# First load, zero products, evictions and normalisation times of a one-layer hybrid trunk

## The chip, the core and the metric

The kernel runs on one core of a Trainium2 chip. The time is the device time of one execution in microseconds (us); it was taken three times, and the median is the figure that counts. TensorE (PE) multiplies matrices, ScalarE (ACT) and VectorE (DVE) do elementwise work, GpSimd (POOL) adds a few tiles and issues some transfers, SyncE (SP) issues most of the transfers. Each engine executes its own list in order.

## The reference

One layer on x of 512 tokens by 2048 features, all in float32:

```
h  = rms_norm(x, g0)
P  = h @ w_in                    # 2048 x 5632, eleven blocks of 512 columns
y  = concat[A(P), B(P), C(P), D(P)]   # two attentions, a linear recurrence, a gated convolution
x  = x + rms_norm(y @ w_out, g1)      # w_out 2048 x 2048
h  = rms_norm(x, g2)
u  = causal_conv3(h @ w_up)           # w_up 2048 x 8192
x  = x + rms_norm((gelu(u1) * u2) @ w_down, g3)
```

rms_norm divides each token by the root of its mean square over the 2048 features and multiplies by a gain per feature.

## The kernel before

Activations stand features on partitions, tokens along the free axis, in 16 tiles of 128x512. So that float32 accuracy is kept, each operand is split into a rounded part hi and a remainder lo, and a product is made of three matmuls (hi·hi, hi·lo, lo·hi); in the half groups of w_out one matmul takes hi and lo of the activation together, 512 wide, and a second, 256 wide, takes lo of the weight.

Weights stream through `chunk` (line 95). A chunk is 128x1024 of a weight: SyncE loads w_raw (L105), ScalarE rounds it to w_hi (the cast, L106), VectorE subtracts to w_lo (L107). Each of the three has three buffers, so the load of chunk i waits for L107 of chunk i-3, and cast and subtraction of chunk i for the matmuls of chunk i-3. The first chunk is loaded and split in two pieces.

`group` (L132) makes 512 output columns: eight chunks into four PSUM banks, one u for each 128 columns. The last chunk goes bank by bank, and when a bank is complete its eviction `evac` is called with high priority; what `evac` returns is called afterwards in ordinary order. There are two pools of four banks, mm and pa. `tick` counts a quarter of a chunk, and `at(t, f)` puts work f beside tick t. TensorE's order is that of the program; the lists of the other engines are made by a scheduler, which takes high-priority work (loads, casts, subtractions) as early as it can.

Before the first product, TensorE multiplies a tile of zeros twenty times (L70 to L72; a float32 product is two passes, so 40 instructions). `load_x` (L266) loads x on SyncE, two feature tiles at a time after the first two, and splits them (L199 on ScalarE, L200 on VectorE). The squares of x go beside it: ScalarE squares (L282), VectorE sums them into vd (L284, L286). At tick 28, between chunk 6 and chunk 7 of the first group, `norm0` multiplies that sum with ones (L308) and makes the reciprocal root. The parameters (L298) are loaded late, and VectorE's small steps L375 to L392 (negb, la_s, la_q, la_m, lam, sp) need them.

w_out is four groups of columns. Groups 0 and 1 take all 512 tokens at once (PSUM tile of 128x512, both on mm); groups 2 and 3 take one half of the tokens, hf 0 then hf 1, group 2 on mm and group 3 on pa. Evictions of groups 0 and 1 are a scaled copy (L968) and squares (L838). Those of the halves add the two PSUM halves (ScalarE L978, VectorE L979), square (L838; GpSimd sums, L842) and scale by the gain (L964). When the sixteenth square of a half is out, `residual` is put six ticks later: ones times the sums (L852, two terms for hf 0, five for hf 1), a reciprocal root (L207, L210), multiplications (L876), for half of the tiles a transfer that adds onto xs (`accum_op`, L878, GpSimd's queue), for the others an add (L882). `residual` puts squares (L894, L896), `scaled` (L902, and a store of xs to x_d on SyncE, L904) and, 43 ticks on, `norm2` (L911 on TensorE, then L917 and the split L196, L197), which makes the operands of w_up.

Of the kernel before, what the change touches and what calls it, by code (L numbers as in the profile page):

```python
# [23 lines left out]
ALL = slice(0, S)  # L24
# [24 lines left out]
def trunk(ctx: ExitStack, tc: tile.TileContext, xT, params, consts, wgate, w_in, w_out, w_up0, w_up, w_dn, w_dns, out):  # L49
# [18 lines left out]
    idle = const.tile([P, P], F32, name="idle")  # L68
    V.memset(idle, 0.0)
    ps = pa_tile()[:, 0:P]  # L70
    for _ in range(20):
        T.matmul(ps, lhsT=idle, rhs=idle, start=True, stop=True)  # L72


# [20 lines left out]
    def chunk(src, pieces=1, place=None):  # L95
        with tc.high_priority(offset=AHEAD):
            raw = wp.tile([P, 2, S], F32, name="w_raw")
            if place is None:
                hi = wp.tile([P, 2, S], F32R, name="w_hi")
                lo = wp.tile([P, 2, S], F32R, name="w_lo")  # L100
            else:
                hi, lo = place[:, 0:2], place[:, 2:4]
            for i in range(pieces):
                sl = slice(2 * i // pieces, 2 * (i + 1) // pieces)
                w_load.append(nc.sync.dma_start(out=raw[:, sl], in_=src[:, sl]))  # L105
                w_split.append(A.copy(out=hi[:, sl], in_=raw[:, sl]))  # L106
                V.tensor_tensor(out=lo[:, sl], in0=raw[:, sl], in1=hi[:, sl].bitcast(F32), op=ALU.subtract)  # L107
        return hi, lo
# [701 lines left out]
    with ExitStack() as ph:  # L810
# [57 lines left out]
        def residual(hf):  # L868
# [14 lines left out]
            for n, q in enumerate((0, 2, 1, 3)):  # L883
                at(clock[0] + 19 + 5 * hf + 4 * n // 3, lambda n=n, q=q: squares(hf, q, acc, n == 0))
                at(clock[0] + 25 + 5 * hf + 2 * n, lambda q=q: scaled(hf, q))
            at(clock[0] + 43, lambda: norm2(hf, acc))

        def squares(hf, q, acc, first):

# [67 lines left out]
        def out_group(g, hfs, ts, pool_tile):  # L957
            def evac(u, ps):
                k = 4 * g + u
                if len(hfs) == 1:  # L960
                    m = mg[g][hfs[0]][:, u]
                    sum_of(m, ps)
                    last = ss1[hfs[0]].add(m)
                    A.activation(out=m, in_=m, func=AF.Copy, scale=gain(1, k))  # L964
                    if last:
                        at(clock[0] + 6, lambda: residual(hfs[0]))
                else:
                    A.activation(out=mg_t[g // 2][:, g % 2, :, u], in_=ps.rearrange("p (h t) -> p h t", h=2),  # L968
                                 func=AF.Copy, scale=gain(1, k))
                    for hf in hfs:  # L970
                        ss1[hf].add(ps[:, HALVES[hf]])
# [8 lines left out]


        for g in range(2):
            out_group(g, (0, 1), ALL, mm_tile)
        for hf in range(2):
            for g in range(2, 4):
                out_group(g, (hf,), HALVES[hf], mm_tile if g == 2 else pa_tile)
# [525 lines left out]
```

## Time and profile before

| what | value |
|---|---|
| three runs | 1744.21, 1743.61, 1743.55 us; median 1743.61 us |
| the profiled execution | 1741.86 us, of which the span in the profile is 1740.1 us |
| TensorE busy | 1730.1 us of the span, 9168 matmuls |
| VectorE, ScalarE, GpSimd busy | 1253.8, 905.8, 157.8 us |
| granted TensorE clock | full speed over the span |

The profile's engine times overlap. A wait in it is the idle time of an engine just before an instruction, put down to what ended it. On a busy engine each instruction's duration is longer than its step, since one starts before the last is out; what a row of equal instructions takes is read from start to start.

### The profile page before, as it was taken

To read this page: it belongs to the slowest core of one execution; us is meant where nothing else is said; L and a number is where in the kernel's file an instruction comes from. 1 tells how busy PE (TensorE), PEld (TensorE's weight loads), DVE (VectorE), ACT (ScalarE), POOL (GpSimd) and SP (SyncE) were. 2 spreads that over 40 slices of the span, in tenths; PEclk is the share of its full clock that TensorE was granted. 3 is DMA by queue.
4 is the path that set the end of the run, shared out by engine and by line. 5 is a ranking of instruction groups with operands and counts; after the bars stand their busy time and mean duration, and the time that the engine had idled before them with its cause. 6 is when DMAs were issued, how large, how long until landed. Compare 5 with 4: busy or idle time off the path is not lost.

```text
span 1740.1 us, 24385 instructions
## 1 busy us (share of the span) xinstructions
PE 1730.1 (99%) x9168; PEld 1482.5 (85%) x9168; DVE 1253.8 (72%) x1949; ACT 905.8 (52%) x1367; POOL 157.8 (9%) x227
## 2 busy tenths in 40 slices
PE   9999999999999999999999999999999999999998
PEld 8778888888888888899988888888888888888886
DVE  7885587666556425799898988888878887776335
ACT  6443577665334334776655555555555573334342
POOL 0000011100000011100011111111111001110120
PEclk9999999999999999999999999999999999999999
DMA  7224222242223625775789888888888768888322
GB/s 258 84 99 147 92 79 79 79 158 97 85 86 97 230 97 181 233 234 180 208 230 243 236 224 247 225 230 223 228 239 226 210 198 232 217 201 296 102 91 97
DMA packets 96014, 304.43 MB, mean 175 GB/s; under 512 B 10356, under 2 KB 14708, under 8 KB 95896
## 3 DMA queue, kind: packets, MB, share of 16 engines
q1 hardware_dynamic: 79768, 245.19, 42.1%
q0 software_dynamic: 15552, 56.63, 17.4%
q8 instruction: 72, 1.18, 0.3%
q10 hardware_dynamic: 576, 1.05, 0.2%
q14 instruction: 46, 0.38, 0.1%
HBM read 262.45 MB, written 21.24 MB: 163 GB/s over the span
## 4 chain that ended last, share of the span: by engine, by line
PE 92%; DVE 3%; DMA 2%; ACT 2%; issue 1%; SPq 0%; POOL 0%; ACTq 0%; DVEq 0%; POOLq 0%
PE mm L164 32%; PE mm L1113 27%; PE mm L1118 14%; PE pa L164 5%; PE pa L156 2%; PE mm L128 2%; PE mm L130 2%; PE mm L129 2%; PE mm L156 1%; PE pa L611 1%; DMA w_raw<-in_w_out_dram 1%; DVE w_lo L107 1%; DVE vd L286 1%; PE pa L718 1%; ACT w_hi L106 0%
## 5 line engine op out<-in xcount | busy, mean ns | idle before, releaser
L107 DVE TENSOR_TENSOR w_lo<-w_raw,w_hi 128x1024 fp32r<-128x1024 f32 (+1 forms) x195 | 238.5, 1224 | 234.6 <-PE mm L164 117.3
L106 ACT CAST w_hi<-w_raw 128x1024 fp32r<-128x1024 f32 (+1 forms) x195 | 203.5, 1044 | 264.0 <-PE mm L164 174.1
L164 PE MATMUL mm<-a,w_hi 128*128 128x512 f32 (+1 forms) x1504 | 338.2, 375 | 0.0
L164 PEld LDWEIGHTS mm<-a,w_hi 128*128 128x128 f32 x1504 | 266.7, 188 | 50.9 <-issue 1.8
L1113 PE MATMUL mm<-a,w_hi 128*128 128x512 f32 x1088 | 272.6, 392 | 0.0
L1081 ACT CAST w_hi<-w_raw 128x1024 fp32r<-128x1024 f32 x145 | 152.3, 1050 | 196.0 <-PE mm L1113 154.9
L1113 PEld LDWEIGHTS mm<-a,w_hi 128*128 128x128 f32 x1088 | 195.6, 189 | 35.3 <-issue 0.2
L1082 DVE TENSOR_TENSOR w_lo<-w_raw,w_hi 128x1024 fp32r<-128x1024 f32 x145 | 177.0, 1221 | 29.9 <-ACT w_hi L1081 29.3
L164 PE MATMUL mm<-a,w_lo 128*128 128x512 f32 (+1 forms) x752 | 180.4, 377 | 0.0
L1118 PEld LDWEIGHTS mm<-a,w_lo 128*128 128x128 f32 x1088 | 148.4, 190 | 10.6
L1118 PE MATMUL mm<-a,w_lo 128*128 128x256 f32 x1088 | 151.7, 282 | 0.0
L164 PEld LDWEIGHTS mm<-a,w_lo 128*128 128x128 f32 x752 | 131.8, 189 | 22.3
L1113 PE MATMUL mm<-xs,w_hi 128*128 128x512 f32 x576 | 144.3, 392 | 0.2 <-DVE ub L1179 0.2
L1081 ACT CAST w_hi<-mg 128x1024 fp32r<-128x1024 f32 x82 | 85.6, 1044 | 85.0 <-PE mm L1113 82.5
L1113 PEld LDWEIGHTS mm<-xs,w_hi 128*128 128x128 f32 x576 | 103.6, 189 | 19.0 <-DVE ub L1179 0.4
L1082 DVE TENSOR_TENSOR w_lo<-mg,w_hi 128x1024 fp32r<-128x1024 f32 x82 | 100.1, 1220 | 21.4 <-ACT w_hi L1081 21.4
L1113 PE MATMUL mm<-mg,w_hi 128*128 128x512 f32 x352 | 88.1, 392 | 0.0
L1118 PEld LDWEIGHTS mm<-xs,w_lo 128*128 128x128 f32 x576 | 78.6, 190 | 5.6
L1179 DVE TENSOR_TENSOR ub<-ub,mm 128x256 f32<-128x256 f32 x196 | 81.2, 414 | 0.0
L1118 PE MATMUL mm<-xs,w_lo 128*128 128x256 f32 x576 | 80.3, 282 | 0.0
L1281 DVE TENSOR_TENSOR m<-m,mm 128x256 f32<-128x256 f32 x112 | 46.5, 416 | 37.0 <-PE mm L1118 37.0
L1113 PEld LDWEIGHTS mm<-mg,w_hi 128*128 128x128 f32 x352 | 63.3, 189 | 11.3
(332 smaller groups left out, 2709.1 us busy)
## 6 DMA issues: line engine op xcount, KB each, us to landing
w_raw<-in_w_up_dram SPq DMA_DIRECT2D x115, 512.0 KB, 5.3
w_raw<-in_w_in_dram SPq DMA_DIRECT2D x87, 512.0 KB, 3.4
mg<-in_w_up_dram SPq DMA_DIRECT2D x54, 512.0 KB, 4.4
w_raw<-in_w_out_dram SPq DMA_DIRECT2D x48, 512.0 KB, 3.6
w_raw<-in_w_dn_dram SPq DMA_DIRECT2D x32, 512.0 KB, 4.2
mg<-in_w_up_dram POOLq DMA_DIRECT2D x27, 512.0 KB, 7.8
w_raw<-in_w_up_dram POOLq DMA_DIRECT2D x27, 512.0 KB, 8.9
w_raw<-mg POOLq DMA_DIRECT2D x27, 512.0 KB, 6.0
```

Of the source, the lines that this page charges most:

```text
L106: w_split.append(A.copy(out=hi[:, sl], in_=raw[:, sl]))
L107: V.tensor_tensor(out=lo[:, sl], in0=raw[:, sl], in1=hi[:, sl].bitcast(F32), op=ALU.subtract)
L128: T.matmul(ps, lhsT=sh, rhs=mh, start=first, stop=False)
L129: T.matmul(ps, lhsT=sh, rhs=ml, start=False, stop=False)
L156: T.matmul(pss[u][:, 0:256] if low else pss[u].rearrange("p (a t) -> p a t", a=2), lhsT=(wh, wl)[low][:, kk, us], rhs=both[k][:, 0, ts] if ...
L164: T.matmul(pss[u], lhsT=a, rhs=b, start=c == 0 and kk == 0 and not low and i == 0, stop=False)
L1081: w_split.append(A.copy(out=by4(hi), in_=v))
L1082: V.tensor_tensor(out=by4(lo), in0=v, in1=by4(hi).bitcast(F32), op=ALU.subtract)
L1113: T.matmul(ps.rearrange("p (a t) -> p a t", a=2), lhsT=hi[:, k * P:(k + 1) * P], rhs=tops[name][k], start=first and k == 0, stop=False, **kw)
L1118: T.matmul(ps[:, 0:256], lhsT=lo[:, k * P:(k + 1) * P], rhs=tops[name][k][:, 0], start=False, stop=k == 7, **kw)
L1179: taken.append(V.tensor_tensor(out=t, in0=t, in1=ps[:, 256:512], op=ALU.add))
L1281: V.tensor_tensor(out=t, in0=t, in1=part, op=ALU.subtract if i else ALU.add)
```

## The change

Five edits. (1) The very first weight piece is loaded by ScalarE's queue, all others by SyncE's as before. (2) Ten zero products in place of twenty. (3) In the half groups the squares and the scaled copy are returned by `evac` and so are issued in ordinary order; only the sum of the two PSUM halves stays at high priority. (4) The group with g = 1 of w_out takes its four banks from pa. (5) `residual` stands eight ticks after the last square and `norm2` 44 ticks after `residual`, in place of 6 and 43.

```
@@ -68,7 +68,7 @@
-    for _ in range(20):
+    for _ in range(10):
         T.matmul(ps, lhsT=idle, rhs=idle, start=True, stop=True)
@@ -102,7 +102,9 @@
-                w_load.append(nc.sync.dma_start(out=raw[:, sl], in_=src[:, sl]))
+                queue = nc.sync if w_load else nc.scalar
+                w_load.append(queue.dma_start(out=raw[:, sl], in_=src[:, sl]))
@@ -883,7 +885,7 @@
-            at(clock[0] + 43, lambda: norm2(hf, acc))
+            at(clock[0] + 44, lambda: norm2(hf, acc))
@@ -960,10 +962,13 @@
                     sum_of(m, ps)
-                    last = ss1[hfs[0]].add(m)
-                    A.activation(out=m, in_=m, func=AF.Copy, scale=gain(1, k))
-                    if last:
-                        at(clock[0] + 6, lambda: residual(hfs[0]))
+                    def more():
+                        last = ss1[hfs[0]].add(m)
+                        A.activation(out=m, in_=m, func=AF.Copy, scale=gain(1, k))
+                        if last:
+                            at(clock[0] + 8, lambda: residual(hfs[0]))
+                    return more
@@ -980,7 +985,7 @@
-            out_group(g, (0, 1), ALL, mm_tile)
+            out_group(g, (0, 1), ALL, pa_tile if g else mm_tile)
```

The scheduler's lists change with it. Lines behind the edits have other numbers in the changed kernel: L107 becomes L109, L106 L108, L286 L288, L308 L310, L838 L840, L978 L983, L964 L968.

VectorE in the first group, around the subtraction for chunk 7; vd is the sum of squares, la_m and la_q small parameters. Before:

```order
L286 TENSOR_TENSOR vd<-vd,t_302 128x512
L387 TENSOR_SCALAR la_m<-la_m 128x4
L286 TENSOR_TENSOR vd<-vd,t_313 128x512
L386 TENSOR_TENSOR la_m<-la_m,la_q 128x4
L286 TENSOR_TENSOR vd<-vd,t_316 128x512
L107 TENSOR_TENSOR w_lo<-w_raw,w_hi 128x1024
L286 TENSOR_TENSOR vd<-vd,t_323 128x512
```

Now:

```order
L388 TENSOR_TENSOR la_m<-la_m,la_q 128x4
L288 TENSOR_TENSOR vd<-vd,t_292 128x512
L389 TENSOR_SCALAR la_m<-la_m 128x4
L109 TENSOR_TENSOR w_lo<-w_raw,w_hi 128x1024
L288 TENSOR_TENSOR vd<-vd,t_303 128x512
L388 TENSOR_TENSOR la_m<-la_m,la_q 128x4
L401 SCALAR_TENSOR_TENSOR lam<-lm 128x1
L288 TENSOR_TENSOR vd<-vd,t_306 128x512
```

The subtraction stands two sums of squares earlier: after the first L288 and not after the third.

VectorE at the end of the sum of squares, ahead of `norm0`; the subtraction here is that of the second group's first chunk. Before:

```order
L286 TENSOR_TENSOR vd<-vd,t_443 128x512
L387 TENSOR_SCALAR la_m<-la_m 128x4
L286 TENSOR_TENSOR vd<-vd,t_446 128x512
L386 TENSOR_TENSOR la_m<-la_m,la_q 128x4
L286 TENSOR_TENSOR vd<-vd,t_485 128x512
L387 TENSOR_SCALAR la_m<-la_m 128x4
L286 TENSOR_TENSOR vd<-vd,t_488 128x512
L386 TENSOR_TENSOR la_m<-la_m,la_q 128x4
L107 TENSOR_TENSOR w_lo<-w_raw,w_hi 128x1024
L387 TENSOR_SCALAR la_m<-la_m 128x4
```

Now:

```order
L288 TENSOR_TENSOR vd<-vd,t_433 128x512
L389 TENSOR_SCALAR la_m<-la_m 128x4
L288 TENSOR_TENSOR vd<-vd,t_436 128x512
L388 TENSOR_TENSOR la_m<-la_m,la_q 128x4
L288 TENSOR_TENSOR vd<-vd,t_475 128x512
L109 TENSOR_TENSOR w_lo<-w_raw,w_hi 128x1024
L288 TENSOR_TENSOR vd<-vd,t_478 128x512
L389 TENSOR_SCALAR la_m<-la_m 128x4
L388 TENSOR_TENSOR la_m<-la_m,la_q 128x4
```

The subtraction was behind the last sum of squares and is now ahead of it.

ScalarE in the last group of the second half (g = 3, hf = 1) while the banks of group 2 are evicted; s, f are squares of the first half's new x, q squares of the evicted tile. The casts of chunks 2 and 3 are in it. Before:

```order
L978 COPY mg<-mm 128x256
L902 ACTIVATE mg<-xs,par 128x256
L978 COPY mg<-mm 128x256
L838 ACTIVATE q_5968<-mg 128x256
L838 ACTIVATE q_5978<-mg 128x256
L964 ACTIVATE mg<-mg,par 128x256 x2
L838 ACTIVATE q_5993<-mg 128x256
L978 COPY mg<-mm 128x256
L964 ACTIVATE mg<-mg,par 128x256
L106 CAST w_hi<-w_raw 128x1024
L838 ACTIVATE q_6003<-mg 128x256
L106 CAST w_hi<-w_raw 128x1024
```

Now:

```order
L896 ACTIVATE f_5927<-xs 128x512
L983 COPY mg<-mm 128x256
L896 ACTIVATE f_5934<-xs 128x512
L983 COPY mg<-mm 128x256
L896 ACTIVATE f_5937<-xs 128x512
L983 COPY mg<-mm 128x256
L108 CAST w_hi<-w_raw 128x1024
L983 COPY mg<-mm 128x256
L840 ACTIVATE q_5952<-mg 128x256
L840 ACTIVATE q_5962<-mg 128x256
L968 ACTIVATE mg<-mg,par 128x256
L108 CAST w_hi<-w_raw 128x1024
```

The cast of chunk 2 stood behind the squares and scalings of three evictions; now it is behind the copies alone, with the first square behind it.

ScalarE at the evictions of that same group, where the first chunks of w_up are cast. Before:

```order
L978 COPY mg<-pa 128x256 x3
L838 ACTIVATE q_6227<-mg 128x256
L838 ACTIVATE q_6236<-mg 128x256
L964 ACTIVATE mg<-mg,par 128x256 x2
L838 ACTIVATE q_6245<-mg 128x256
L978 COPY mg<-pa 128x256
L964 ACTIVATE mg<-mg,par 128x256
L106 CAST w_hi<-w_raw 128x1024
L838 ACTIVATE q_6254<-mg 128x256
```

Now:

```order
L968 ACTIVATE mg<-mg,par 128x256
L983 COPY mg<-pa 128x256
L108 CAST w_hi<-w_raw 128x1024
L198 CAST a_94<-mg 128x2x256
L840 ACTIVATE q_6226<-mg 128x256
L108 CAST w_hi<-w_raw 128x1024
L198 CAST a_94<-mg 128x2x256
L968 ACTIVATE mg<-mg,par 128x256
L840 ACTIVATE q_6235<-mg 128x256
L840 ACTIVATE q_6244<-mg 128x256
```

Two casts and two splits of norm2 now stand between the last copies and the last two squares.

## Rows read from the trace of the kernel before

**Rows 1.** The page: busy time of each engine, and the granted clock in 40 slices.

```profile
PE 1730.1 (99%) x9168; PEld 1482.5 (85%) x9168; DVE 1253.8 (72%) x1949; ACT 905.8 (52%) x1367; POOL 157.8 (9%) x227
...
PEclk9999999999999999999999999999999999999999
```

**Rows 2.** The waits of TensorE over the whole span, by line and by what ended them: us in total, times, longest.

```profile
PE pa L156 <- ACT w_hi L106: 1.4, 1, 1.4
...
PE mm L156 <- ACT q L838: 0.7, 1, 0.7
PE pa L852 <- ACT q L838: 0.4, 1, 0.4
```

**Rows 3.** The start on TensorE: timeline rows (start, us, instruction, count) of the zero products, the first real product and the second chunk's first; and of a table by stretches the one from 1.0 to 4.9 us (length, busy time and instructions of PE, granted clock, DMA share, GB/s).

```profile
1.19 6.48 PE L72 MATMUL pa<-idle 128*128 128x128 f32 x40 [1.19 <-DVE la_m L384]
7.42 0.48 PE L128 MATMUL mm<-a,w_hi 128*128 128x512 f32 x1
...
12.96 3.79 PE L164 MATMUL mm<-a,w_hi 128*128 128x512 f32 x16
...
1.00:4.90 3.90, 3.71 (x17) 1.00 0.70 201
```

**Rows 4.** The start on the other engines, timeline rows: SyncE's issues, ScalarE's first split and cast, VectorE's split of feature tiles 2 and 3.

```profile
1.25 0.42 SPq L274 DMA_DIRECT2D t<-in_xT_dram  x1
1.71 0.43 SPq L105 DMA_DIRECT2D w_raw<-in_w_in_dram  x1
...
4.02 0.72 ACT L199 ACTIVATE a<-t,par 128x512 fp32r<-128x512 f32 x1 [1.93 <-DMA t<-in_xT_dram]
4.96 0.62 ACT L106 CAST w_hi<-w_raw 128x512 fp32r<-128x512 f32 x1 [0.22 <-DMA w_raw<-in_w_in_dram]
...
11.26 1.41 DVE L200 SCALAR_TENSOR_TENSOR a<-t,par,a 128x512 fp32r<-128x512 f32 x2
```

**Rows 5.** TensorE in the first group, timeline rows: the lo part of chunk 4, that of chunk 6, and norm0.

```profile
32.91 1.98 PE L164 MATMUL mm<-a,w_lo 128*128 128x512 f32 x8
...
43.79 1.98 PE L164 MATMUL mm<-a,w_lo 128*128 128x512 f32 x8
46.08 1.12 PE L308 MATMUL pa<-vd,con 128*128 128x512 f32 x2 [0.31 <-DVE vd L286]
```

**Rows 6.** VectorE in the same stretch, timeline rows: the first step that needs the parameters, the subtraction for chunk 7, the sum behind it, the last sum, and the subtraction for the next group.

```profile
31.02 0.17 DVE L375 TENSOR_SCALAR negb<-par 128x8 f32<-128x8 f32 x1 [0.25 <-DMA par<-in_params_dram]
...
34.98 1.23 DVE L107 TENSOR_TENSOR w_lo<-w_raw,w_hi 128x1024 fp32r<-128x1024 f32 x1
36.12 0.69 DVE L286 TENSOR_TENSOR vd<-vd,t 128x512 f32<-128x512 f32 x1
...
45.33 0.69 DVE L286 TENSOR_TENSOR vd<-vd,t 128x512 f32<-128x512 f32 x1
...
46.01 1.22 DVE L107 TENSOR_TENSOR w_lo<-w_raw,w_hi 128x1024 fp32r<-128x1024 f32 x1
```

**Rows 7.** The start of group 2 of w_out on TensorE, timeline rows: chunk 0, its hi part in two pieces and its lo part, and chunk 1.

```profile
651.16 1.52 PE L156 MATMUL mm<-a,w_hi 128*128 128x512 f32 x6
653.37 0.73 PE L156 MATMUL mm<-a,w_hi 128*128 128x512 f32 x2 [0.69 <-ACT q L838]
653.94 1.10 PE L156 MATMUL mm<-a,w_lo 128*128 128x256 f32 x8
654.88 2.00 PE L156 MATMUL mm<-a,w_hi 128*128 128x512 f32 x8
656.72 1.11 PE L156 MATMUL mm<-a,w_lo 128*128 128x256 f32 x8
```

**Rows 8.** TensorE in group 3 of the second half, timeline rows: chunk 1, chunk 2, norm2 of the first half, and chunk 4.

```profile
722.85 2.00 PE L156 MATMUL pa<-a,w_hi 128*128 128x512 f32 x8
...
727.19 2.10 PE L156 MATMUL pa<-a,w_hi 128*128 128x512 f32 x8 [1.38 <-ACT w_hi L106]
...
733.53 1.03 PE L911 MATMUL mm<-s,con 128*128 128x256 f32 x4
734.20 2.20 PE L156 MATMUL pa<-a,w_hi 128*128 128x512 f32 x8
```

**Rows 9.** ScalarE ahead of chunk 2's cast in that group, timeline rows.

```profile
721.41 0.63 ACT L894 ACTIVATE f<-xs 128x512 f32<-128x512 f32 x1
721.94 0.35 ACT L978 COPY mg<-mm 128x256 f32<-128x256 f32 x1
722.20 0.64 ACT L894 ACTIVATE f<-xs 128x512 f32<-128x512 f32 x1
...
726.11 1.03 ACT L106 CAST w_hi<-w_raw 128x1024 fp32r<-128x1024 f32 x1
```

**Rows 10.** The adding transfer of the first half's residual on GpSimd's queue and the store behind it on SyncE's, timeline rows.

```profile
706.99 1.02 POOL L878 DMA_DIRECT2D xs<-mg  x1 [7.88 <-DMA w_raw<-in_w_out_dram]
...
713.83 0.33 SPq L904 DMA_DIRECT2D x_d<-xs  x1
```

**Rows 11.** The second half's residual: TensorE's last term, and the square that it waits for, timeline rows.

```profile
751.75 0.70 PE L852 MATMUL pa<-q,con 128*128 128x256 f32 x2 [0.42 <-ACT q L838]
...
751.29 0.41 ACT L838 ACTIVATE q<-mg 128x256 f32<-128x256 f32 x1
```

**Rows 12.** The first groups of w_up, one stretch of a table by stretches: length, then busy us and instructions of PE, PEld, DVE, ACT and POOL, granted clock, DMA share, GB/s.

```profile
800.00:840.00 40.00, 40.00 (x335) 40.00 (x335) 39.95 (x43) 26.30 (x31) 0.00 (x0) 1.00 0.60 197
```

## The prediction

> **What bounds the kernel now.** I read the page's busy times and granted clock first [rows 1]. TensorE is busy for 1730.1 of 1740.1 us at full clock, so only the ten idle microseconds of TensorE can be won, besides the zero products that count as busy. The table of TensorE's waits comes next [rows 2]: besides the 1.2 us ahead of the first instruction its largest entries are 1.4, 0.7 and 0.4 us. Then the timeline of TensorE around each entry, with the engine named there. What is to be seen: every edit aims at one entry or at the start, no entry is above 1.4 us, and everywhere else TensorE works without a gap. A change of 0.2% is 3.49 us (about what a measurement of this kernel can tell from no change), and nearly all that there is would have to go at once to pass it.
>
> The sum is made against the profiled execution, 1741.86 us, with 1.76 us outside its span. The median of the runs is 1743.61, 1.75 us above it; I add the sum to the median.
>
> **The start: ten products and the first piece on ScalarE's queue.** The 40 passes begin at 1.19 and the first real product starts at 7.42 [rows 3], although its operands are there much earlier: ScalarE's split of x starts at 4.02, the cast at 4.96 [rows 4]. Only the zero products hold it. Up to 4.9 us, 17 passes take 3.71 us, 0.218 each; the other 23 fit into the 2.5 us up to 7.4, 0.11 each. So the fast pace begins at about 4.9, and 20 passes end near 4.9 + 3 x 0.11 = 5.2. The first real product can start some 2.2 us earlier; the third then waits a little for w_lo.
>
> The lead does not stay at 2.2, since the transfers do not follow. SyncE takes 0.46 us from one issue to the next (1.25 to 1.71) [rows 4]; with one issue fewer on SyncE every later load of the start can come about s = 0.46 us earlier, if the loads are not held by bandwidth. ScalarE and VectorE work through these loads in their order, and the second chunk needs feature tile 3 split, which VectorE ends at 11.26 + 1.41 = 12.67 [rows 4]; after, at 12.2. Matmuls follow each other every 0.227 us here (48 in the two chunks from 32.91 to 43.79 [rows 5]); the second chunk began at 12.96 [rows 3] and its fourth matmul, the first with that operand, three later at 13.64. So TensorE's lead through the first group is 13.64 - 12.25, **about 1.4 us** (0.9 if s is nothing).
>
> Apart from these numbers: the Trainium skill ("DMA: Bandwidth & Descriptors", section "Issuing engines are not separate DMA queues") says that transfers issued by several engines share the same sixteen engines, and that only the issuing is spared. The stretch to 4.9 us shows a DMA share of 0.70 already. By that rule s is one issue and no more; a queue with a bandwidth of its own would let w_raw land together with x at 4.0, 0.9 us ahead of its cast at 4.96.
>
> **The lead meets norm0.** Norm0 starts at 46.08 after a wait of 0.31 us for the last sum of squares [rows 5]. So VectorE already decides there, and a lead of TensorE buys only a longer wait. VectorE's sums begin late (its first step on the parameters starts at 31.02, released by their transfer) and are dense from there [rows 6]. The change makes their list longer ahead of norm0. Before, the subtraction for chunk 7 is behind three sums and starts at 34.98, the next sum at 36.12, and the last sum at 45.33: eleven steps and one more subtraction of 1.14, so (45.33 - 36.12 - 1.14)/11 = 0.73 us a sum with its small step. From 34.98 to 46.08 are 11.10 us. The order of the changed kernel, shown above, has that subtraction after the first sum, so that two more stand behind it, and it has the second group's first subtraction (46.01 in the trace, behind the last sum [rows 6]) ahead of the last sum. That adds 2 x 0.61 to 0.73 and 1.14, together 2.35 to 2.6 us, to the 11.10.
>
> When may the subtraction for chunk 7 start? It writes the buffer that TensorE reads in the lo part of chunk 4, which ends about 34.72 (32.91 + 8 x 0.227) [rows 5]; it began 0.26 later. With the lead that becomes 33.6, and VectorE, which began on the parameters at 31.02 (0.46 earlier now), reaches it at about 34.98 - 0.46 - 2 x 0.73 = 33.1 and waits for it. So norm0 comes at 33.6 + 11.1 + 2.45 = 47.1 in place of 46.08: **+1.05 us**, and TensorE, done with chunk 6 at about 44.3, waits some 2.7 us there, the longest wait of the kernel. Behind norm0 TensorE is bound by its own work again for hundreds of microseconds, so this passes to the end. Bounds: +1.7 (2.6 - 0.9), if the lead is 0.9 us and the two sums cost 0.73, to -1.4, if the sums are not what holds (the first rival).
>
> **The second group on other banks: -0.94.** Group 2's first chunk needs its four banks, which group 1 used before; the fourth is freed by ScalarE's squares, and TensorE waits 0.69 us [rows 7]. The hi part of that chunk goes from 651.16 to 653.94, 2.78 us, where the next takes 1.84 (654.88 to 656.72). With group 1 on pa, group 2's banks were last used by group 0, long evicted. Group 1 itself takes pa, which nobody else holds then, and group 3 of the first half comes 22 us after. Nothing is late next: the first cast of group 2 is done before. I take all of 0.94; the lower end is the wait as listed, 0.69.
>
> **The evictions in ordinary order: -2.34.** In group 3 of the second half TensorE waits 1.38 us for chunk 2's cast [rows 8]. ScalarE casts at 726.11, behind the squares and gains of group 2's evictions, busy without a gap from 721.41 on [rows 9]. Chunks 1 to 3 take 11.35 us (722.85 to 734.20); three undisturbed ones, each 1.84 + 0.94 [rows 7], and norm2's matmuls (733.53 to 734.20) take 9.01: 2.34 lost. Now the cast of chunk 2 stands ahead of all those squares and gains, behind the copies (order above): three squares at 0.53 and three copies at 0.26 from start to start [rows 9] after chunk 1's cast put its end near 724.5, where TensorE asks for it at 725.6; chunk 2's w_lo, then chunk 3, follow in time. I take all of it; the other end is nothing (third rival).
>
> The same edit helps the second half's residual, which waits 0.42 us for its last square [rows 11]. Two casts and two splits are put ahead of squares there, but TensorE comes earlier by the lead just won, and the residual two ticks later; the last square ends about 750, before the fifth term's turn. **-0.42**; the other end is nothing.
>
> **Residual and norm2 later.** Their matmuls are the same and cost TensorE nothing more. Residual comes two ticks, 2 x 2.78/4 = 1.4 us, later. Behind it: GpSimd's adding transfer, issued at 706.99 and ended when SyncE's store follows at 713.83, 6.84 later [rows 10], now about 715.2. SyncE issues in order, so the loads behind that store wait 1.4 longer: chunk 2's load goes at about 715.7 and lands near 721.4, ahead of its cast. Hidden by 2 us. Then norm2's splits must be ready for the first chunks of w_up, which TensorE now reaches 2 us earlier, while norm2 itself starts half a microsecond later. VectorE is full there, 39.95 of 40 us from 800 on [rows 12]; I allow **+0.3 us** in small waits (0 to 0.9).
>
> Sum: -0.94 - 2.34 - 0.42 + 1.05 + 0.3 = **-2.3 us**: 1739.5 for a profiled execution, 1743.61 - 2.3 = **1741.3** for the median, 0.13% below.
>
> **The rivals.**
>
> First, the start's lead is kept: norm0 is not held by VectorE because the sums run ahead (parameters early, subtraction for chunk 7 later than the list makes it look). Then -1.4 in place of +1.05: -4.8 us, 1738.8, faster. Against it: VectorE held norm0 already by 0.31 us with a shorter list [rows 5]. Chance 0.13.
>
> Second, slower: VectorE becomes the bound from norm2 to the second pair of w_up groups. It is busy 39.95 of 40 us there [rows 12]; if its work starts with norm2's split and leaves no slack, all that TensorE wins before 738 us is only waited off, and the three extra ticks ahead of norm2 (3 x 0.70 = 2.1) and 0.4 for the splits come on top: +1.05 + 2.1 + 0.4 = +3.5, 1747.1. It decides if norm2's multiplications start over 0.5 us later than before and VectorE is still full at 800 us with TensorE waiting for w_lo. Against it: the changed list puts w_up's subtractions ahead of that work, and TensorE did not wait for VectorE there before. Chance 0.08.
>
> Third, the evictions do not free the cast: what holds it at 726 is the load (behind the store on SyncE's queue) or the squares of the new x, now 1.4 us later. Then 2.34 stays lost: -0.94 - 0.42 + 1.05 + 0.3 = 0.0, 1743.6. For it: ScalarE has the same work in these 8 us. Chance 0.13.
>
> Fourth, the longer wait ahead of norm0 costs clock. The waits of up to 1.4 us before left it at full speed [rows 1, 2]; 2.7 us has no row. The start shows the price of a slow stretch: 17 passes at 0.218 in place of 0.11 lose 1.9 us. Then 1743.2. The Trainium skill ("TensorE: Matmul & The Clock Gate", "What's actually happening") says that an idle stretch brings the half clock back, and no run here shows it after the start. Chance 0.08.
>
> **How the numbers follow.** The forecast has 0.58. The range goes from the first rival's 1738.6 up to 1745.0, which holds the fourth, and the third with +1.7 at norm0 and 0.9 of small waits (1743.61 - 0.94 - 0.42 + 1.7 + 0.9 = 1744.9); what it leaves out is the second rival and some of the first. Faster by over 0.2%: the first rival and the forecast's low end, 0.18. Slower: most of the second, 0.06. Within: 0.76.
>
> **What would show it.** Right: the first real product at 5.2, the second chunk's lo near 12.2; a wait of about 2.7 us for vd ahead of norm0 at 47; no wait at the start of group 2; none for a cast in group 3 of the second half; clock full throughout; small waits at the first w_up groups. Wrong: norm0 starting below 45, which makes it faster, or waits of several microseconds for w_lo between 740 and 850.

## The result and the profile after

| kernel | median of its runs | lowest to highest |
|---|---|---|
| before | 1744.09 us (8 runs) | 1742.85 to 1745.35 |
| changed | 1749.05 us (8 runs) | 1746.81 to 1751.03 |

The ratio is 1.0027, with a 95% interval of 1.0017 to 1.0038: 3.0 to 6.6 us slower, where 2.3 us faster was forecast, and outside the range. The profiled execution of the changed kernel took 1749.16 us (span 1747.4), close to its median. That of before took 1741.86, which is 2.2 us below the median of its eight runs; so of the 7.3 us between the two spans some two are a quick execution of before, and the comparison is better made place by place.

TensorE's waits in the changed kernel, all of them (us in total, times, longest), beside [rows 2]:

```profile
PE pa L310 <- DVE vd L288: 2.7, 1, 2.7
PE mm L1118 <- DVE ub L1184: 1.7, 2, 1.5
PE mm L166 <- DVE a L199: 1.4, 2, 0.7
PE pa L72 <- DVE la_m L386: 1.2, 1, 1.2
PE mm L913 <- DVE s L898: 1.1, 1, 1.1
PE pa L854 <- ACT q L840: 0.7, 1, 0.7
PE pa L166 <- ACT w_hi L108: 0.7, 1, 0.7
PE mm L166 <- DVE ub L1184: 0.7, 1, 0.7
PE pa L854 <- ACT ys L840: 0.2, 1, 0.2
```

The waits for w_hi in a half group and for q ahead of group 2 are gone; that for vd ahead of norm0 and that for q at the residual have grown, and five others have come. The start on TensorE (timeline rows), to be held against [rows 3]:

```profile
1.19 4.63 PE L72 MATMUL pa<-idle 128*128 128x128 f32 x20 [1.19 <-DVE la_m L386]
5.83 0.80 PE L130 MATMUL mm<-a,w_hi 128*128 128x512 f32 x1
6.62 0.57 PE L131 MATMUL mm<-a,w_hi 128*128 128x512 f32 x1
7.02 0.39 PE L132 MATMUL mm<-a,w_lo 128*128 128x512 f32 x1
...
12.01 3.79 PE L166 MATMUL mm<-a,w_hi 128*128 128x512 f32 x16
...
31.96 1.98 PE L166 MATMUL mm<-a,w_lo 128*128 128x512 f32 x8
...
42.84 1.98 PE L166 MATMUL mm<-a,w_lo 128*128 128x512 f32 x8
47.53 1.91 PE L310 MATMUL pa<-vd,con 128*128 128x512 f32 x2 [2.72 <-DVE vd L288]
48.45 1.42 PE L130 MATMUL mm<-a,w_hi 128*128 128x512 f32 x1
49.67 0.63 PE L131 MATMUL mm<-a,w_hi 128*128 128x512 f32 x1
50.09 0.63 PE L132 MATMUL mm<-a,w_lo 128*128 128x512 f32 x1
```

The twenty passes end at 5.8 and not 5.2: these, too, run at the slow pace. The second chunk starts at 12.01, 0.95 ahead of before. Norm0 then waits 2.72 us, as worked out, and starts 1.45 later than before [rows 5]; but its two passes last 1.91 us in place of 1.12, and the products behind it are 0.42 us apart (49.67 to 50.09) where 0.23 is normal. The table by stretches shows the granted clock of the five microseconds behind it, 0.66, a mean of its two levels of 1.2 and 2.4 GHz (columns as in rows 12):

```profile
47.00:52.00 5.00, 4.46 (x11) 2.88 (x12) 3.16 (x11) 2.41 (x3) 0.00 (x0) 0.66 0.32 107
```

VectorE ahead of norm0 (timeline), against [rows 6]:

```profile
34.03 1.23 DVE L109 TENSOR_TENSOR w_lo<-w_raw,w_hi 128x1024 fp32r<-128x1024 f32 x1 [1.52 <-ACT ones_r L305]
35.17 0.69 DVE L288 TENSOR_TENSOR vd<-vd,t 128x512 f32<-128x512 f32 x1
...
45.66 1.22 DVE L109 TENSOR_TENSOR w_lo<-w_raw,w_hi 128x1024 fp32r<-128x1024 f32 x1
46.80 0.68 DVE L288 TENSOR_TENSOR vd<-vd,t 128x512 f32<-128x512 f32 x1
```

The subtraction for chunk 7 starts at 34.03, though VectorE was free 1.52 us before. The engine named in that row is not the one that held it: TensorE's last product on the buffer, in the lo part of chunk 4, is over at 33.77 (31.96 + 8 x 0.227, timeline above), and the subtraction follows 0.26 later, as before. From there to norm0 are 13.5 us, as worked out (11.10 and 2.45).

At w_out both gains are there (TensorE's timeline; [rows 7, 8]), and what follows takes them:

```profile
654.16 1.98 PE L158 MATMUL mm<-a,w_hi 128*128 128x512 f32 x8
...
656.92 2.00 PE L158 MATMUL mm<-a,w_hi 128*128 128x512 f32 x8
...
727.68 2.00 PE L158 MATMUL pa<-a,w_hi 128*128 128x512 f32 x8
...
733.26 2.00 PE L158 MATMUL pa<-a,w_hi 128*128 128x512 f32 x8
...
736.84 1.10 PE L913 MATMUL mm<-s,con 128*128 128x256 f32 x4 [1.10 <-DVE s L898]
...
755.12 1.13 PE L854 MATMUL pa<-q,con 128*128 128x256 f32 x4 [0.75 <-ACT q L840]
```

Group 2's first chunk takes 2.76 us where it took 3.72. Chunk 2 of group 3 starts without a wait, and chunk 4 at 733.26, where before chunk 3 ended at 733.53: the lateness of 2.0 us at 657 has become a lead of 0.27. Norm2 then waits 1.10 us for the sum of squares. ScalarE shows why (timeline):

```profile
718.25 0.63 ACT L896 ACTIVATE s<-xs 128x512 f32<-128x512 f32 x1 [4.25 <-DMA xs<-mg]
...
741.84 0.46 ACT L209 ACTIVATE f<-mm,eps 128x256 f32<-128x256 f32 x1
...
745.89 0.63 ACT L198 CAST a<-mg 128x512 fp32r<-128x512 f32 x1 [2.21 <-DVE mg L919]
```

It is idle for 4.25 us until the adding transfer lands at 718.2, 4.4 later than in [rows 10]. The transfer is no slower than before (6.8 us); GpSimd issues it 4.45 later, at 711.44. Of this, 2.0 are TensorE's lateness at 655 and 1.4 the two ticks of `residual`. Norm2's reciprocal root comes at 741.84 and the first split for w_up at 745.89, where before these two were (ScalarE's timeline)

```profile
737.42 0.45 ACT L207 ACTIVATE f<-mm,eps 128x256 f32<-128x256 f32 x1
...
740.55 0.62 ACT L196 CAST a<-mg 128x512 fp32r<-128x512 f32 x1 [1.28 <-DVE mg L917]
```

so 4.4 and 5.3 us earlier. (The 0.9 between them is a weight's subtraction, which VectorE now does at 742.67 between norm2's steps.) TensorE reaches w_up only one microsecond later than before, at 746.6, and from there it waits for splits, casts and evictions. Behind 803, VectorE is full (the table by stretches):

```profile
803.00:854.00 51.00, 49.46 (x395) 48.53 (x394) 50.87 (x56) 32.11 (x42) 2.61 (x3) 1.00 0.63 199
```

It was full there before, too ([rows 12]), and TensorE did not wait. The difference lies ahead of that stretch: from 733 to 806 VectorE waits 10.9 us in all, 3.0 of them for norm2's reciprocal roots on ScalarE (2.1 for the first half's, 0.9 for the second's); before it waited 8.4 us from 733 to 803, and never for a root. Between the matmuls that start at 798 and at 850 before, it is then busy for 52.4 us in place of 50.6.

Place by place, the start of one and the same matmul in the changed kernel less that in before: +3.07 at the second chunk of the second group (55.60 against 52.53), +2.04 at 655, -0.26 at chunk 3 of group 3 (730.7), +1.01 at the first chunk of w_up (745.6), +4.66 at 798 and +6.34 at 850. So the start costs 3.07, the banks win 1.03, the evictions 2.30, and 6.6 us are lost between 731 and 850.

### The profile page after: what moved, and what is told of

The parts are those of the page before. It is cut to its first block, busy times and chain, and to the rows that moved or that the text cites. A ratio compares the mean times of both kernels' runs of the same rounds, so it can differ in the third digit from the quotient of the medians.

```text
span 1747.4 us, 24343 instructions
## 1 busy us (share of the span) xinstructions
PE 1731.6 (99%) x9148; PEld 1482.0 (85%) x9148; DVE 1255.3 (72%) x1949; ACT 904.7 (52%) x1367; POOL 161.9 (9%) x227
## 4 chain that ended last, share of the span: by engine, by line
PE 89%; DVE 5%; issue 3%; DMA 1%; ACT 1%; POOL 0%; ACTq 0%; DVEq 0%; POOLq 0%; SPq 0%
PE mm L166 29%; PE mm L1118 26%; PE mm L1123 13%; PE pa L166 5%; PE pa L158 2%; PE mm L158 2%; PE mm L130 2%; PE mm L131 2%; PE mm L132 2%; DVE w_lo L109 1%; PE pa L613 1%; DMA w_raw<-in_w_out_dram 1%; PE pa L720 1%; DVE a L199 0%; DVE vd L288 0%
## 5 line engine op out<-in xcount | busy, mean ns | idle before, releaser
L109 DVE TENSOR_TENSOR w_lo<-w_raw,w_hi 128x1024 fp32r<-128x1024 f32 (+1 forms) x195 | 239.4, 1227 | 241.0 <-PE mm L166 89.7
L108 ACT CAST w_hi<-w_raw 128x1024 fp32r<-128x1024 f32 (+1 forms) x195 | 203.5, 1045 | 268.3 <-PE mm L166 149.9
L166 PE MATMUL mm<-a,w_hi 128*128 128x512 f32 (+1 forms) x1392 | 312.2, 375 | 2.0 <-DVE a L199 1.4
L166 PEld LDWEIGHTS mm<-a,w_hi 128*128 128x128 f32 x1392 | 245.6, 188 | 49.3 <-issue 1.8
L1118 PEld LDWEIGHTS mm<-a,w_hi 128*128 128x128 f32 x1088 | 195.7, 189 | 36.9 <-DVE ub L1184 1.7
L166 PE MATMUL mm<-a,w_lo 128*128 128x512 f32 (+1 forms) x696 | 166.9, 376 | 0.0
L1123 PEld LDWEIGHTS mm<-a,w_lo 128*128 128x128 f32 x1088 | 148.4, 190 | 10.6
L166 PEld LDWEIGHTS mm<-a,w_lo 128*128 128x128 f32 x696 | 121.4, 189 | 20.2
```

The lines of the kernel that those rows point to most:

```text
L166: T.matmul(pss[u], lhsT=a, rhs=b, start=c == 0 and kk == 0 and not low and i == 0, stop=False)
L1118: T.matmul(ps.rearrange("p (a t) -> p a t", a=2), lhsT=hi[:, k * P:(k + 1) * P], rhs=tops[name][k], start=first and k == 0, stop=False, **kw)
L1123: T.matmul(ps[:, 0:256], lhsT=lo[:, k * P:(k + 1) * P], rhs=tops[name][k][:, 0], start=False, stop=k == 7, **kw)
```

## The experiments

Each kernel ran in five rounds beside the kernel before. "Difference" is its median less that of before in the same rounds (before: 1743.8 to 1744.0 in 29 to 33 runs). Below stands for most of them the same difference in starts as above, taken from the profiled execution, at the same six places. Two things are to be kept in mind: kernels with twenty products differ by up to 1.2 us at the first place already (before 52.53, residual_8 53.35, no_start 53.72), since the slow pace of the zero products lasts longer in some executions; and behind 850 other waits come and go between executions, most of them under 2 us.

| kernel | 52.5 | 654.9 | 730.7 | 745.6 | 798 | 850 | difference |
|---|---|---|---|---|---|---|---|
| changed | +3.07 | +2.04 | -0.26 | +1.01 | +4.66 | +6.34 | +5.0 |
| start_only | +3.02 | +3.00 | +3.02 | +3.00 | +4.86 | +4.72 | +5.3 |
| warm | +1.58 | +0.58 | -1.75 | -0.76 | +1.19 | +2.86 | +3.5 |
| subs_behind | -1.02 | -1.04 | -0.50 | -0.50 | +0.96 | +1.47 | +1.2 |
| all_subs | -0.88 | -1.84 | -4.17 | -3.36 | -0.85 | +0.84 | +2.2 |
| no_ticks | +3.07 | +2.08 | +1.16 | +1.28 | +4.91 | +4.72 | +3.6 |
| no_start | +1.19 | +0.23 | -2.08 | -1.34 | +0.39 | +2.07 | +1.2 |
| evict_only | +0.25 | +0.21 | -0.71 | -0.72 | +2.71 | +2.52 | +1.4 |
| ticks_only | +0.36 | +0.35 | -0.21 | -0.23 | +2.08 | +3.77 | +2.1 |
| residual_8 | +0.82 | +0.79 | +0.38 | +0.37 | +0.36 | +3.70 | +2.4 |
| banks_only | +0.51 | -0.49 | -0.31 | -0.32 | +0.18 | +0.32 | +0.5 |

### The start

**start_only**: `range(20)` to `range(10)`, and the first piece on ScalarE's queue.

> The kernel before with ten zero products and the first piece on ScalarE's queue, nothing else. If the start explains its part of the loss (norm0 waits 2.7 us for VectorE's longer list and TensorE's clock falls in that wait), this kernel is about 3.1 us slower than before: norm0 starts 1.4 to 1.5 us later, and the first chunk of the second group 3.1 us later. Rival: the wait is there but the clock is a mishap of one profiled execution; then it is 1.4 us slower. If neither, the kernel is up to 1 us faster.

Measured: ratio 1.0035 (1.0021 to 1.0050). Norm0 waits 2.7 us, and the second group is 3.02 late. The start explains its part and loses it without the other edits. The median is 5.3 us above that of before, 2.2 more than expected. The profiled execution, the slowest of the six (1755.45 us), loses 1.9 more between 745 and 798, and 8.8 behind 850, most of it at two waits of 1.7 and 3.0 us near 1446 and 1475 with slow products behind the second; how much of this the median has is not shown.

**queue_only** and **ten_only**: one of the two each.

> The kernel before with the first weight piece on ScalarE's queue alone; twenty zero products stay. Its list for VectorE has the subtraction for chunk 7 after the first sum of squares and the next group's ahead of the last sums, as in the changed kernel. If that list makes the loss, norm0 starts 2 us or more later than before although the start has no lead, TensorE waits some 2.5 us and more there, its clock falls, and the kernel is 3 to 4 us slower than before. Rival: the lead of TensorE makes the wait; then this kernel is within 1 us of before.

> The kernel before with ten zero products alone. If VectorE's list makes the loss, and the list stays much as it was, norm0 starts within 0.3 us of before, TensorE's lead of 0.5 to 0.9 us is waited off there, the clock stays up, and the kernel is within 0.5 us of before. Rival: any lead makes the wait long and costs clock; then it is 1.5 us slower or more.

Measured: 0.9998 (0.9990 to 1.0007) and 1.0027 (1.0017 to 1.0038), the opposite of both expectations. The expectation of queue_only misread its list: in the trace seven squares are in the sum before the subtraction for chunk 7, and the sums end at 44.8, so that norm0 does not wait. That of ten_only has one sum ahead of it (VectorE's timeline, then TensorE's):

```profile
32.30 0.69 DVE L286 TENSOR_TENSOR vd<-vd,t 128x512 f32<-128x512 f32 x1
34.65 1.22 DVE L107 TENSOR_TENSOR w_lo<-w_raw,w_hi 128x1024 fp32r<-128x1024 f32 x1 [1.66 <-PE mm L164]
35.79 0.69 DVE L286 TENSOR_TENSOR vd<-vd,t 128x512 f32<-128x512 f32 x1
...
45.62 1.22 DVE L107 TENSOR_TENSOR w_lo<-w_raw,w_hi 128x1024 fp32r<-128x1024 f32 x1
46.75 0.68 DVE L286 TENSOR_TENSOR vd<-vd,t 128x512 f32<-128x512 f32 x1
```

```profile
48.21 1.12 PE L308 MATMUL pa<-vd,con 128*128 128x512 f32 x2 [2.78 <-DVE vd L286]
```

VectorE stands idle 1.66 us ahead of that subtraction, until TensorE has read the buffer, with the sums behind it. Either edit makes the scheduler order VectorE's work anew, once well and once badly. Taken by themselves the two outcomes are those of the rivals, though: no lead and no wait, a lead and a wait. What decides between list and lead is subs_behind, below, which has the lead and another order.

**warm**: the changed kernel, and ahead of norm0's product in the same bank

```
            for _ in range(10):
                T.matmul(ps[:, 0:P], lhsT=idle, rhs=idle, start=True, stop=True)
```

> The changed kernel with ten zero products (20 passes, 2.2 us at full speed) ahead of norm0's product, in the time in which TensorE waits. If the clock falls because TensorE is idle there, they keep it up: norm0 still starts at 47.5, its passes and the next products run at 0.23 and not 0.42 to 0.6 us, and the kernel is 1.6 us faster than the changed one. If the clock has another cause, the products come for nothing or cost up to 1 us.

Measured: 1.0019 (1.0011 to 1.0028). Norm0 starts at nearly the same time (47.70), the clock stays up, and the second group is 1.5 us earlier than in the changed kernel (timeline of TensorE):

```profile
44.82 2.40 PE L310 MATMUL pa<-idle 128*128 128x128 f32 x20
47.70 1.12 PE L311 MATMUL pa<-vd,con 128*128 128x512 f32 x2 [0.49 <-DVE vd L287]
48.26 0.80 PE L129 MATMUL mm<-a,w_hi 128*128 128x512 f32 x1
48.90 0.39 PE L130 MATMUL mm<-a,w_hi 128*128 128x512 f32 x1
49.12 0.39 PE L131 MATMUL mm<-a,w_lo 128*128 128x512 f32 x1
```

This shows that the slow products came from TensorE's idle time, and 1.5 us as its price. The medians differ by the same 1.5 us.

**sums_first**: the two edits of the start, the banks, and all small steps on the parameters (L375 and the others) held behind the last sum.

> The two edits of the start and group 1 on the other banks, and VectorE's small steps on the parameters only after the last sum of squares, so that the sums need not wait for the parameters' transfer. If VectorE's list ahead of norm0 is what eats the lead, norm0 starts at 44.9 (46.08 less the lead of 0.95 and the wait of 0.31), the clock stays up, and with the banks' 0.94 the kernel is 2.0 to 2.3 us faster than before. Rival: the sums are held by something else (ScalarE's squares, the subtraction for chunk 7); then norm0 stays at 46 or later and the kernel is 1 us faster or less.

Measured: 1.0024 (1.0015 to 1.0034), norm0 at 47.38 after a wait of 2.77. The sums began earlier, one was done by 30.7, and VectorE then waited 3.15 us for chunk 7's buffer. From 35 on they follow each other every 0.73 us without any small step between, since each needs the one before. The parameters are not what holds.

**subs_behind**: the two edits of the start, and

```
+                behind = {9: 8, 10: -1}.get(len(w_split))
+                with tc.issue_after(sums[behind].ins) if behind else ExitStack():
                     V.tensor_tensor(out=lo[:, sl], in0=raw[:, sl], in1=hi[:, sl].bitcast(F32), op=ALU.subtract)
```

where sums is the list of VectorE's sums: chunk 7's subtraction stands behind the tenth square, the second group's first behind the last.

> The two edits of the start (ten products, first piece on ScalarE's queue), and in VectorE's list the subtraction for chunk 7 behind the tenth feature tile's square and the second group's first subtraction behind the last sum. If the place of these two subtractions in VectorE's list makes the wait ahead of norm0 (chunk 7's has to wait for TensorE, and the sums behind it follow each other every 0.73 us), the last sum is done by 44, norm0 starts at 44.8, 1.26 us earlier than before, TensorE does not wait and its clock stays up; against the kernel with the two edits alone that is 4.3 us less at norm0. Rival: the sums are held by ScalarE's squares; then norm0 stays at 46 or later. What is left of the lead at 850 us is open, since norm2's part took 0.5 to 1.7 us from other kernels that came earlier or later.

Measured (TensorE's timeline):

```profile
45.09 1.12 PE L311 MATMUL pa<-vd,con 128*128 128x512 f32 x2 [0.19 <-DVE vd L289]
```

Norm0 starts 0.99 earlier than before, and the second group 1.02; against start_only that is 4.04. The lead is won by the place of two instructions. At 850, however, the kernel is 1.47 us later than before, so 2.5 us are lost on the way, and the ratio is 1.0009 (1.0000 to 1.0018).

**all_subs**: the same in the changed kernel.

> The changed kernel, all five edits, with those two subtractions in the same places. By the theory of VectorE's list the start's 3.07 us turns into a gain of 1.26: 4.3 us less at 50 us than the changed kernel, and 3.5 to 4.5 us less in all, about before or 1 us slower. Rival: an earlier TensorE only waits longer at norm2 and the first chunks of w_up; then it is 2 us less than the changed kernel or nothing.

Measured: 1.0013 (1.0003 to 1.0023), 3.95 us better than the changed kernel at the first place, 5.5 at 850, 2.8 in the medians. At 730.7 it is 4.17 us ahead of before, and at 850 0.84 behind.

### From w_out to w_up

**no_start**: the changed kernel without the two edits of the start.

> The changed kernel without the two edits of the start. If the start costs 3.1 us, this kernel is 3.1 us faster than the changed one, 1.5 to 3 us slower than before: the gains of 0.94 and 2.31 are there and some 4.5 us of waits between 733 and 803 us. Rival: those waits come from TensorE's place against VectorE after the late start; then they shrink and the kernel is 2 to 3 us faster than before.

Measured: 1.0006 (0.9998 to 1.0015). The gains are those of the changed kernel (0.96 at the banks, 2.31 at the evictions), and 4.15 us are given back from 731 to 850. So most of those waits do not come from the late start. Without it the adding transfer lands at 716.0 (2.2 later than before) and norm2's root comes at 738.17 (0.75 later).

**no_ticks**: the changed kernel with 6 and 43 ticks.

> The changed kernel with residual and norm2 at 6 and 43 ticks as before. If the later ticks make the waits ahead of norm2, of the first chunks of w_up and of the second half's residual, this kernel is 4 us or more faster than the changed one, about 0 to 1 us faster than before even with the start's 3.1. Rival: the evictions' new order makes them, by casts and splits ahead of squares; then it is within 1 us of the changed kernel.

Measured: 1.0021 (1.0012 to 1.0030), 1.5 us better in the medians and neither case in full. The waits at norm2, at w_up's splits and casts and at 850 are gone. In their place the two residuals wait, for GpSimd's sum (1.1) and for a square (TensorE's timeline, and a stretch of the table):

```profile
754.34 2.93 PE L853 MATMUL pa<-q,con 128*128 128x256 f32 x6 [2.60 <-ACT q L839]
```

```profile
738.00:768.00 30.00, 27.40 (x186) 25.30 (x186) 28.48 (x44) 21.10 (x37) 1.76 (x2) 0.94 0.56 176
```

and the clock falls once more behind the wait of 2.6 us.

**evict_only** and **ticks_only**: the evictions' order alone; the ticks alone.

> The kernel before with the half groups' squares and scalings in ordinary order alone (residual and norm2 at 6 and 43). If the squares, put behind the casts, come late for residual when it stays at 6 ticks, the 2.2 us at the casts of group 3 are won and both residuals wait, 1 us and 2.6 us or more with a loss of clock: 0.5 to 2 us slower than before. Rival: the waits in the kernel without later ticks came from its late start; then it is 1.5 to 2.5 us faster.

> The kernel before with residual at 8 and norm2 at 44 ticks alone. If the chain from residual over the adding transfer, the squares of the new x and norm2 to the first operands of w_up has no slack, two ticks (1.4 us) and one more come back as waits of TensorE between 727 and 850: 1 to 3 us slower than before. Rival: the ticks are covered, and the waits of the changed kernel come from the evictions' order; then it is within 0.5 us of before.

Measured: 1.0006 (0.9997 to 1.0015) and 1.0014 (1.0005 to 1.0023). The evictions' order alone wins 0.9 up to 731 (1.4 us of its gain go to the first residual) and loses 3.4 at the second residual, where the clock falls behind waits of 1.7 and 0.3 us for squares (TensorE's timeline, and a stretch of the table):

```profile
751.49 1.13 PE L852 MATMUL pa<-q,con 128*128 128x256 f32 x4 [1.74 <-ACT q L838]
```

```profile
738.00:768.00 30.00, 27.98 (x194) 26.11 (x193) 29.10 (x46) 19.04 (x34) 1.76 (x2) 0.94 0.58 169
```

The ticks alone lose 4.0 us between 731 and 850: 2.0 of waits for splits, and 1.5 for an evicted column of w_up at 850.

**residual_8**: residual at 8 ticks, norm2 43 behind it.

> The kernel before with residual at 8 ticks alone, norm2 43 ticks behind it as before. If residual's two ticks are what makes the waits between 738 and 850 us of the kernel with both ticks (3.8 us by 850 us), this one has them nearly all: 2.5 to 3.8 us by 850 us, the wait of 1.5 us for an evicted column of w_up at 850 us among them. Rival: norm2's one tick brings VectorE's list over an edge; then this kernel is within 1.5 us of before at 850 us and that wait is not there.

Measured: 1.0010 (1.0001 to 1.0019). Nothing is lost up to 798 and 3.3 us from there to 850, where TensorE waits for VectorE:

```profile
841.15 0.39 PE L130 MATMUL pa<-a,w_lo 128*128 128x256 f32 x1 [1.27 <-DVE w_lo L107]
850.81 2.12 PE L1113 MATMUL mm<-a,w_hi 128*128 128x512 f32 x8 [1.19 <-DVE ub L1179]
```

Two ticks of residual are enough for the loss at its end; norm2's third decides where ahead of 850 a part of it shows. The wait at 850 is in every profile with residual at 8 ticks (changed, warm, no_start, all_subs, ticks_only, residual_8), and in none of the others of the table, whatever their lead. A wait of the same kind of 1.4 to 1.5 us stands at 888, however, in banks_only, mended and mended_late_start, which have residual at 6.

**banks_only**: group 1 on pa alone.

> The kernel before with group 1 of w_out on the other banks alone. The wait of 0.69 us at the start of group 2 goes and 0.94 us with it, and nothing later takes it: 0.9 to 1.0 us faster than before. Rival: TensorE, earlier against VectorE and ScalarE, waits longer for the second half's residual and for the first chunks of w_up; then it is within 0.3 us of before.

Measured: 1.0004 (0.9995 to 1.0012), the rival's case. 1.00 us is won at 654, and 0.8 of it is gone by 850.

### A version meant to beat both

**norm2_40** (norm2 40 ticks behind residual), **mended** (both edits of the start, the two subtractions behind the sums, the banks, norm2 at 40; evictions and residual as before) and **mended_late_start** (the same without the edits of the start):

> The kernel before with norm2 40 ticks behind residual in place of 43, nothing else. If the chain over norm2 to w_up's operands has no slack but TensorE waits for none of it in the kernel before, the three ticks (2.1 us) bring little by themselves: 0 to 0.5 us faster, by the second half's residual, whose last square then stands less late. Rival: norm2's sum isn't done then and TensorE waits for it: up to 1 us slower.

> The two edits of the start with VectorE's two subtractions behind the sums, group 1 on the other banks, and norm2 at 40 ticks; evictions and residual as before. Leads of 1.0 and 0.95 us at 660 us. If an earlier norm2 gives the chain the slack that it lacks, 1 to 2 us are left at 850 us, and the kernel is 1 to 2 us faster than before. Rival: the second half's residual and w_up's first chunks take the leads back all the same (ScalarE and VectorE have the same work in the same time); then it is within 0.5 us of before or slower.

> The same without the two edits of the start: twenty products, the first piece on SyncE's queue, VectorE's two subtractions behind the sums, banks, norm2 at 40. The lead is 0.3 from norm0 and 0.95 from the banks. With slack in norm2's chain it is 0.8 to 1.2 us faster than before, without it within 0.3 us.

Measured: 0.9999 (0.9990 to 1.0008), 0.9991 (0.9983 to 1.0000) and 0.9998 (0.9989 to 1.0007). mended has a median of 1741.83 against 1743.92 us, 2.1 us less, and its interval ends at no change: faster, but at the edge of what was measured. Its profile does not show where the gain comes from. That execution took 1745.81 us, 4.0 above the median, and was a late one at the start, since the slow pace lasted to 10.5 us there (products 0.43 us apart). Norm0 waits 0.2 us in it, and TensorE keeps its place from 654.9 to 745.6 (-0.08 at both, so no lead) and is 0.37 behind at 798. Mended_late_start was expected 0.8 to 1.2 us faster if norm2 at 40 gives the chain slack; it is 0.1 faster, the case without slack. So mended's time came as expected, but the reason given for it is not borne out.

## Why the prediction was wrong

**The second group's banks, the evictions: right.** Forecast 0.94 and 2.34 for TensorE at the place; measured 1.03 and 2.30 in the changed kernel, 0.96 and 2.31 in no_start.

**Norm0: the mechanism was right, two sizes and one rival were not.** The prediction saw that the two subtractions in VectorE's list make norm0 late, and the wait, 2.7 us, is 2.72. Subs_behind, which has the lead and the other order, confirms that it is the list and not the lead. The lead was 0.95 and not 1.4, so that +1.05 became +1.45: the split that was to bound it is done at 12.13 (forecast 12.2), but TensorE's own products, started at 5.8 and slow, lasted to 12.01. (The 12.25 in the sum is 12.21 by its own rows, and the range's 1738.6 is the first rival's 1738.8; neither matters.) The larger error is the fourth rival, to which 0.08 was given: the clock fell, for another 1.62 us (priced at 1.9); warm gives 1.5 of it back. The prediction argued that no wait of up to 1.4 us had cost clock; the row for 2.7 us was missing and was then taken for "no". The runs have the rows that were missing: waits of 2.6 to 3.0 us cost clock in every profile that has them (changed, start_only, ten_only, sums_first, no_ticks). The Trainium skill ("TensorE: Matmul & The Clock Gate", "What's actually happening"), cited there, had said that an idle stretch brings the half clock back, and the trace agrees: the granted clock is 0.66 in the five microseconds behind norm0.

**"Residual and norm2 later", with "+0.3 us in small waits", and "-0.42": the step that failed.** Between 731 and 850 the changed kernel loses 6.6 us, where the prediction had a gain of about 0.1. It put a price on each wait at its own place, and checked for each cast whether it comes in time. It did not ask what becomes of the chain as a whole: evictions' squares, residual, adding transfer, squares of the new x, norm2, splits, w_up's first chunks, all in ScalarE's and VectorE's lists. That chain ends the stretch, not the cast. Evict_only, ticks_only and no_ticks show the exchange: casts ahead of squares win 2.3 us in group 3, and the squares then come late for residual, or residual is put later and the chain ends later. The transfer, forecast to land 1.4 later, landed 4.4 later with the late start and 2.2 without it (no_start). "Hidden by 2 us" held for the load behind the store; it did not hold for the chain behind the same transfer. The second rival, VectorE as the bound up to 850, comes near to this, with a price of 3.5 us and a chance of 0.08, and its point of decision was met: norm2's root starts 4.4 us later (0.75 in no_start). That residual's two ticks alone bring the wait at 850 is shown by residual_8. That VectorE's list carries it is read from the traces and not shown by a run of its own: VectorE was just as full there before, without a wait.

**The sum.** By places: +3.07 - 1.03 - 2.30 + 6.6 = +6.3 at 850 in one execution, and +5.0 in the medians.

**What stays open.** The waits behind 850 differ from execution to execution, and each kernel has one profile; so what they do to a median is not known. Evict_only's and ticks_only's losses do not add up to that of both (2.5 and 3.8 against 2.1 with the banks), so how the two share the chain's lateness is argued from waits and not shown. A kernel without the adding transfer was not tried.

## What to carry to other kernels

Where a scheduler makes the lists, read the list of the engine that a product waits for after any edit, even of one transfer: an instruction that has to wait for TensorE, put ahead of a chain of dependent sums, can cost more than the edit is worth, and one explicit order mends it. A wait that is moved along a saturated chain is not removed; take its price at the chain's end and not where the wait stood. And an idle stretch of TensorE, longer than any that the trace shows at full clock, has to be priced with the slow products behind it.

## What the runs showed of the hardware

- Behind waits of 2.6 to 3.0 us TensorE's next products were 0.42 to 0.43 us apart in place of 0.23, and ten zero products in the wait kept the pace. Shorter waits were not all harmless. Behind one of 1.85 us in warm (at 1443) the products were 0.43 us apart, and behind two close together, of 1.74 and 0.28 us, in evict_only those of 256 columns were 0.21 apart in place of 0.12; behind 1.65 us in queue_only and 1.67 in start_only they kept the pace. In group 3 (columns as in rows 12) sums_first waits 1.71 us, mended_late_start 1.91 and queue_only 2.29, and their rows there, with granted clocks of 1.00, 0.86 and 0.86, are, in this order:

```profile
724.00:736.00 12.00, 10.12 (x59) 8.51 (x58) 10.57 (x14) 10.56 (x24) 3.59 (x4) 1.00 0.73 239
```

```profile
724.00:736.00 12.00, 10.09 (x50) 8.59 (x49) 9.83 (x12) 11.04 (x24) 3.74 (x4) 0.86 0.70 217
```

```profile
724.00:736.00 12.00, 9.71 (x48) 8.13 (x47) 10.16 (x12) 11.12 (x24) 3.60 (x4) 0.86 0.64 213
```

- The slow pace at the start does not end at the same time in each execution: 4.9 us in the profile of before, about 7 in that of the changed kernel, 10.5 in mended. The granted clock's column reads 1.00 in these stretches all the same, so the pace has to be read from the products.
- One small instruction of 0.15 us between two dependent sums on VectorE cost nothing: 0.73 us a sum with it (before) and without (sums_first, seven in 5.1 us).
